# Rewriting the expert part of a two-block transformer kernel: a fixed order per pair of experts, a float32 gather from x, and eighteen weight places

## The chip, the cores and the metric

The kernel runs on one core of a Trainium2 chip, as one program. The metric is the device time of one execution in microseconds (us). Before the change three executions took 1468.20, 1471.01 and 1473.86 us; the median is 1471.01 us. The execution that the profiler recorded took 1472.58 us.

## What is computed

The input is 256 tokens of 1024 float32 features. Two layers of a first block (sparse attention, gated linear attention, spatial gating, and a feed-forward part) are followed by a second block: an attention layer and a mixture of 32 experts, of which each token uses two. The change concerns the mixture and the norm behind it.

```python
def hier_moe(h, w_group, b_group, w_router, b_router, w_e_gate, w_e_up, w_e_down):
    ...
    g_top = jnp.argmax(g_logits, axis=-1)                  # one of 4 groups
    ...
    e_w, e_idx = lax.top_k(jax.nn.softmax(e_logits, axis=-1), TOP_K)   # 2 of its 8 experts
    ...
    for e in range(N_EXPERTS):                             # 32
        a = jax.nn.silu(hf @ w_e_gate[e]) * (hf @ w_e_up[e])     # 1024 -> 512
        out = out + gates[:, e:e + 1].astype(hf.dtype) * (a @ w_e_down[e])   # 512 -> 1024
...
x = x + mixed @ w_out[l]
x = x + hier_moe(rmsnorm_2(x, g_ffn[l]), ...)
return rmsnorm_2(x, g_final)
```

The weights are float32. An expert has 6 MiB of them, the 32 experts together 201.3 MB.

## The kernel before

**Dense parts.** Everything ahead of the mixture multiplies by dense weights. SP's queue loads them into raw places of 8 KB per partition. ScalarE (ACT) casts each piece to a rounded high half `whi`, VectorE (DVE) subtracts to get the low half `wlo`, and TensorE (PE) makes three products of the halves with the halves of the activations (`h_hi`, `h_lo` and others). The tiles `x`, `h_hi`, `h_lo`, the raw places and the arena (one large tile that is cut into working tiles) stand in one pool, `con`; `whi` and `wlo` stand in the pool `split` behind it.

**The experts' weights.** The experts are taken in 16 pairs, q = 0 to 15. A pair has 12 units of 1 MiB: eight for the gate and up matrices (two experts, two matrices, two halves h of the 1024 rows) and four for the down matrices. `plan2` lists the units in the order in which SP loads them: the rows and the downs of a pair in turn, except that the rows of pair 15 stand ahead of the downs of pair 14. `Stream.pump` issues a load as soon as a place is free, and `Stream.free` gives a place back when PE has read it. Eight loads can be in flight, since an issue also waits for the load that is eight before it. The places are the 7 raw ones, 5 that `open_raw("right")` opens, 3 that `open_raw("left")` opens in the second half of `mix2` when `split` is closed, and `LENT` = 3 that `route` lends from the arena for one unit each: 18 units before any expert has run.

**The routing.** While `mix2` ends, `t_xg` makes transposed tokens for the router's logits, and rows of x times the gain (`xgr`) for the gather. `route` then picks each token's two experts by a chain of small VectorE operations. Between them `h_rows` scales `xgr` by the norm's factor and splits it into `h_hi` and `h_lo`, with GpSimd (POOL) and ACT.

**The experts' work.** Experts hold up to 32 tokens (`CAP`). For a batch of four pairs (8 experts) `t_batch` builds one-hot tables from the places, gathers the tokens by 32 products of `h_hi` and `h_lo` with them, builds gated one-hot tables by 24 small operations and transposes these for the way back (`gt`). A pair's gate and up products go into one psum bank of four 32-row strips, banks 4 and 5 in turn. `t_act` makes the activation and transposes it, `emit_down` does the down products into `Y`, and every second pair `emit_scatter` adds `Y` to the tokens in four psum banks. An `If` for experts with more than 32 tokens (`overflow`) stands in pair 15. `last_norm` ends the program.

**What sets the order.** The order is that of the instructions as they are recorded. `t_batch`, `t_act` and `t_most` are side tasks: at each `S.tick()` a planner (`Side`), with a clock of its own for each engine and the numbers of `LAST`, decides whether their next step is recorded; `S.until(...)` records the rest at the latest possible place. `emit_down(q - 1)` is recorded between the two halves of the rows of pair q.

All of these operations pass through one helper, so they carry the line number L257 in the profile; groups are told apart by their tiles.

## Time and profile before

| | |
|---|---|
| median of three executions | 1471.01 us (1468.20 to 1473.86) |
| the profiled execution | 1472.58 us |
| its span, first to last instruction | 1470.8 us |
| mean granted TensorE clock | 0.924 of full speed |
| busy: PE, DVE, ACT, POOL | 1294.8, 740.4, 558.8, 226.4 us |
| read from HBM | 358.1 MB, 244 GB/s over the span |
| the experts' weights | 201.3 MB, loaded from 932 to 1455 us |

The span falls into two parts. Up to about 975 us PE is busy nine tenths of the time or more and the DMA engines about half of it; from there on the DMA engines are busy nine tenths and PE about seven. The averages over the whole span hide this, so the stretches have to be read one at a time. [...]

### The profile page before, as it was taken

How to read it: one execution, taken by the hardware profiler on the slowest of the kernel's cores; microseconds unless marked ns; L12 is line 12 of the kernel's file. 1: busy time of each engine (PE TensorE's matmuls, PEld its weight loads, DVE VectorE, ACT ScalarE, POOL GpSimd, SP SyncE). 2: the span in 40 equal slices, each digit the busy share in tenths (PEclk: the TensorE clock that was granted, in tenths of full speed). 3: DMA queues.
4: the chain of work that ended last, by engine and by line, in shares of the span. 5: the costliest groups of instructions: out<-in, count | busy, mean ns of one | idle time of the engine just before them, and what ended most of it. 6: DMA issues, size and time to landing. Idle time of an engine off the chain costs nothing. (4 is left out here: it accounts for less than half of the span.)

```text
span 1470.8 us, 22896 instructions
## 1 busy us (share of the span) xinstructions
PE 1294.8 (88%) x8791; PEld 966.9 (66%) x8791; DVE 740.4 (50%) x1573; ACT 558.8 (38%) x1167; POOL 226.4 (15%) x348
## 2 busy tenths in 40 slices
PE   8989999999999999999999999978876857776576
PEld 8767999988777899988889999853323212311111
DVE  5587778756587677755766564663021200201001
ACT  5535655555526555555555455431000100100001
POOL 2154111101154111123332210120000000000000
PEclk9999999999999999999999999988987778787778
DMA  9551565556452566566435353697999899899995
GB/s 340 190 184 45 174 200 173 186 159 218 138 168 68 159 186 189 184 193 194 140 116 172 115 173 120 214 379 298 420 421 420 363 420 420 352 420 420 420 417 242
DMA packets 153558, 360.75 MB, mean 245 GB/s; under 512 B 8640, under 2 KB 98240, under 8 KB 128736
## 3 DMA queue, kind: packets, MB, share of 16 engines
q1 hardware_dynamic: 151328, 354.81, 66.1%
q0 software_dynamic: 1328, 3.63, 0.8%
q8 instruction: 71, 1.16, 0.3%
q10 hardware_dynamic: 784, 0.76, 0.2%
q14 instruction: 47, 0.39, 0.1%
HBM read 358.12 MB, written 1.05 MB: 244 GB/s over the span
## 5 line engine op out<-in xcount | busy, mean ns | idle before, releaser
L257 DVE TENSOR_TENSOR wlo<-raw,whi 128x512 fp32r<-128x512 f32 (+3 forms) x560 | 404.9, 730 | 255.4 <-ACT whi L257 243.2
L257 ACT CAST whi<-raw 128x512 fp32r<-128x512 f32 (+3 forms) x560 | 337.7, 606 | 341.6 <-PE psum L257 271.6
L257 PE MATMUL psum<-h_hi,whi 128*128 128x256 f32 x1040 | 296.0, 285 | 3.0 <-ACT whi L257 3.0
L257 PE MATMUL psum<-h_lo,whi 128*128 128x256 f32 x1040 | 290.6, 279 | 0.1
L257 PE MATMUL psum<-h_hi,wlo 128*128 128x256 f32 x1040 | 290.6, 279 | 0.2 <-DVE wlo L257 0.2
L257 PE MATMUL psum<-raw,arena 128*32 128x512 f32 x704 | 181.7, 696 | 58.9 <-DMA raw<-in_w_e_gate_dram 47.5
L257 DVE COPY arena<-psum 128x384 f32<-128x384 f32 (+4 forms) x68 | 38.1, 560 | 346.9 <-ACT arena L257 232.7
L257 PEld LDWEIGHTS psum<-h_hi,whi 128*128 128x128 f32 x1040 | 195.8, 188 | 10.1 <-issue 4.8
L257 PEld LDWEIGHTS psum<-h_lo,whi 128*128 128x128 f32 x1040 | 195.9, 188 | 0.9 <-issue 0.5
L257 PEld LDWEIGHTS psum<-h_hi,wlo 128*128 128x128 f32 x1040 | 195.8, 188 | 0.4 <-DVE wlo L257 0.4
L257 PE MATMUL psum<-raw_right,arena 128*32 128x512 f32 x496 | 143.8, 671 | 24.7 <-DMA raw_right<-in_w_e_gate_dram 17.1
L257 PE MATMUL psum<-whi,h_hi 128*128 128x256 f32 (+3 forms) x448 | 145.7, 325 | 1.4 <-ACT arena_o L257 1.1
L257 PE MATMUL psum<-whi,h_lo 128*128 128x256 f32 (+3 forms) x448 | 138.2, 308 | 0.0
L257 PE MATMUL psum<-wlo,h_hi 128*128 128x256 f32 (+3 forms) x448 | 138.1, 308 | 0.0
L257 PEld LDWEIGHTS psum<-raw,arena 128*32 128x32 f32 x704 | 38.8, 122 | 148.7 <-DMA raw<-in_w_e_gate_dram 62.5
L257 PE MATMUL psum<-raw_left,arena 128*32 128x512 f32 x312 | 110.3, 714 | 26.3 <-DMA raw_left<-in_w_e_gate_dram 20.4
L257 PE MATMUL psum<-arena 64*128 64x256 f32 (+10 forms) x668 | 115.4, 381 | 6.7 <-DVE arena L257 4.7
L257 ACT COPY arena<-psum 128x384 f32<-128x384 f32 (+3 forms) x61 | 32.0, 524 | 221.8 <-PE psum L257 212.4
L257 ACT ACTIVATE arena<-psum 128x256 f32<-128x256 f32 (+3 forms) x38 | 18.1, 476 | 240.7 <-PE psum L257 228.6
L257 POOL TENSOR_TENSOR arena<-arena 128x512 f32<-128x512 f32 (+2 forms) x46 | 49.2, 1079 | 295.6 <-DVE arena L257 286.6
L257 PEld LDWEIGHTS psum<-whi,h_hi 128*128 128x128 f32 x448 | 85.0, 190 | 11.0 <-issue 4.4
L257 PEld LDWEIGHTS psum<-arena 64*128 64x128 f32 (+4 forms) x668 | 63.0, 178 | 42.2 <-issue 22.1
(240 smaller groups left out, 1823.9 us busy)
## 6 DMA issues: line engine op xcount, KB each, us to landing
raw<-in_w_in_dram SPq DMA_DIRECT2D x60, 512.0 KB, 4.9
raw<-in_w_e_up_dram SPq DMA_DIRECT2D x30, 1024.0 KB, 19.8
raw<-in_w_e_down_dram SPq DMA_DIRECT2D x30, 1024.0 KB, 19.9
raw<-in_w_e_gate_dram SPq DMA_DIRECT2D x28, 1024.0 KB, 19.9
raw<-in_w_gate_dram SPq DMA_DIRECT2D x44, 512.0 KB, 4.0
raw<-in_w_up_dram SPq DMA_DIRECT2D x44, 512.0 KB, 5.0
raw_right<-in_w_e_down_dram SPq DMA_DIRECT2D x22, 1024.0 KB, 19.9
raw<-in_w_down_dram SPq DMA_DIRECT2D x20, 1024.0 KB, 5.1
```

The lines of the kernel that those rows point to most:

```text
L257: return f(*args, **kw)
```

## The change

The part from the router to the end is written anew.

- **Order.** The planner is no longer asked in the mixture. A pair is recorded as: rows of half 0, two side steps, rows of half 1, activation, two side steps, its transposes, one side step, its own down products, one side step. The side steps stand in a list: the one-hot tables, four gather steps, the norm factors, the gates (first batch only), two steps for the way back, and the scatters. The list of the next batch is added at the second pair of a batch (at the third pair in the first batch).
- **Gather.** It takes float32 `x` itself (two products of 256 columns per feature group, in float32, where there were four in rounded halves), the gain is applied as the result leaves psum, and the norm's factor of each gathered token is found by eight products with one column per batch and applied in the activation. `h_rows`, `xgr` and the loads of the gain for them are gone.
- **Way back.** The gated tables are made from the one-hot tables by 4 operations per half batch, instead of 24 per batch from the places.
- **Places.** `h_hi` and `h_lo` get a pool of their own, which is closed together with `split`, now at the start of `route`: 5 places instead of 3. The room of the router's tokens becomes another place for good, and `LENT` is 2: 18 places, and 20 units before any expert has run.
- **Warm products.** `route` records `WARM` = 5 float32 products of 512 columns of x whose result is not used, behind the router's logits.
- **Order of the loads.** Rows and downs alternate up to the end, and the last pair's downs are loaded as 8 units of 0.5 MiB (256 rows of 512 columns) so that the columns 0 to 511 come first.
- **End.** Down products, scatter and squares go by halves of the columns; the square's scale takes the place of a division; of the four last scalings ACT does one and DVE three. The final gain is loaded in pair 15, behind the `If`.
- **Addresses.** The arena loses 96 columns. `whi` and `wlo` start where they started (a tile `gap` of 56 columns sees to that); `h_hi` and `h_lo` start 109,512 bytes further on in each partition; x, the raw places and the arena move by 32 bytes modulo 64, or stay.

The core of the diff:

```diff
-LENT = 3
+WARM = 5
+LENT = 2
...
         for q in range(NQ):
             rows(q)
-            if q < NQ - 2:
-                down(q)
-        down(NQ - 2)
-        down(NQ - 1)
+            (down if q < NQ - 1 else last_down)(q)
...
         S.until(("xg", 0), ("xg", 1))
-        S.free = [7]
+
+        self.open_raw("left")
+        self.ar.drop(self.xg)
+        self.st.slots.append(self.room(2048))
         for _ in range(LENT):
-            self.st.lend(self.ar.now(2048), self.ar.drop)
+            self.st.lend(self.room(2048), self.ar.drop)
         self.st.pump()
+        for _ in range(WARM):
+            self.mm(self.ps(0), self.ident, self.x[:, 0, 0:512], True, True)
...
-        for tb in range(2):
-            self.h_rows(tb)
-        self.ar.drop(self.xgr, self.gffn)
...
+        def rows(k2):
+            xe = self.xe[b]
+            ps = self.ps(7 if b else k2).rearrange("p (k c) -> p k c", k=2)
             for i in range(2):
                 k = k2 * 2 + i
                 for tb in range(2):
-                    c0 = tb * D + (k // 4) * 512
-                    c = slice(c0 + k % 4, c0 + 512, 4)
-                    for h in (hi, lo):
-                        self.mm(ps[:, i * 256 : i * 256 + 256], h[:, c], d[:, tb, :], n == 0, n == 3)
+                    c0 = (k // 4) * 512
+                    self.mm(ps[:, i, :], self.x[:, tb, c0 + k % 4 : c0 + 512 : 4], d[:, tb, :], tb == 0, tb == 1)
+            gain = lambda k: self.gp[:, k // 4, k % 4 : k % 4 + 1]
+            k = k2 * 2
+            nc.scalar.activation(out=xe[:, k, :], in_=ps[:, 0, :], func=AF.Copy, scale=gain(k))
+            nc.vector.tensor_scalar(out=xe[:, k + 1, :], in0=ps[:, 1, :], scalar1=gain(k + 1), scalar2=None, op0=ALU.mult)
...
         for q in range(NQ):
...
+            self.emit_rows(q, 0)
+            if q == NQ - 1:
+                with self.tc.If(self.most > CAP):
+                    self.overflow()
...
+            side(2)
+            self.emit_rows(q, 1)
+            if q == 0:
+                side(1)
+            th = self.emit_act(q)
+            side(2)
             if q % 4 == 3:
+                side(99)
                 self.ar.drop(self.xe.pop(b))
+            at = self.emit_at(th)
+            side(1)
...
+            self.emit_down(q, at, None)
+            self.ar.drop(at)
+            if q % 2:
+                todo[:0] = [lambda quad=q // 2, c=c: self.emit_scatter(quad, c) for c in range(2)]
+            side(1)
+        self.last_norm(at)
...
+    def last_norm(self, at):
         for c in range(2):
+            self.emit_down(NQ - 1, at, c)
+            self.emit_scatter(NQ // 2 - 1, c)
             for tb in range(2):
                 ps = self.ps(c * 2 + tb)
-                nc.scalar.activation(out=self.ps(7), in_=ps, func=AF.Square, accum_out=self.ssq[:, tb, c : c + 1])
+                nc.scalar.activation(
+                    out=self.ps(7), in_=ps, func=AF.Square, scale=D ** -0.5, accum_out=self.ssq[:, tb, c : c + 1]
+                )
...
-                if c == 0:
+                if c + tb == 0:
                     nc.scalar.activation(out=o, in_=o, func=AF.Copy, scale=r)
...
-            n = 3
+            self.close("h")
+            n = 5
...
-        N_RAW, N_SPLIT, ARENA = 7, 6, 12032
+        N_RAW, N_SPLIT, ARENA = 7, 6, 11936
```

The order on PE, at the start of the experts, before. `wr` is the router's matrix, `s_9417` the choice of experts, `raw_83` and the like are places with weights; of each run of like rows the first stand here.

```order
L257 MATMUL psum<-wr,arena 128x36 x8
L257 MATMUL psum<-s_9417,tab_67 128x64
L257 MATMUL psum<-s_9417,ones 128x32
L257 MATMUL psum<-onehot,h_hi 128x256
L257 MATMUL psum<-onehot,h_lo 128x256
...
L257 MATMUL psum<-raw_83,arena 32x512
L257 MATMUL psum<-raw_87,arena 32x512
...
L257 MATMUL psum<-onehot,h_hi 128x256
```

And after:

```order
L258 MATMUL psum<-wr,arena 128x36 x8
L258 MATMUL psum<-x,tab_67 128x512 x5
L258 MATMUL psum<-s_9425,tab_67 128x64
L258 MATMUL psum<-s_9425,ones 128x32
L258 MATMUL psum<-onehot,x 128x256 x8
L258 MATMUL psum<-raw_81,arena 32x512
...
L258 MATMUL psum<-onehot,x 128x256 x8
L258 MATMUL psum<-raw_right_9167,arena 32x512
...
L258 MATMUL psum<-rstd,onehot 64x1 x8
L258 MATMUL psum<-tab_67,arena 128x128 x4
```

Before, 16 gather products stand ahead of the first 8 expert products, 8 more gathers and 8 more expert products follow, and then 8 gathers. After, the five warm products stand between the router and the choice; 8 gathers are followed by all 16 expert products of half 0, and 8 more by those of half 1.

The order on PE at the gather of a later batch, before (`tab_67` is the identity of the transposes, `arena 128x512` the scatter):

```order
L257 MATMUL psum<-arena 128x512 x4
L257 MATMUL psum<-raw_left_9340,arena 32x512
...
L257 MATMUL psum<-onehot,h_hi 128x256
...
L257 MATMUL psum<-raw_left_9340,arena 32x512
...
L257 MATMUL psum<-onehot,h_lo 128x256
L257 MATMUL psum<-tab_67,arena 128x128 x8
L257 MATMUL psum<-tab_67,arena 128x64 x4
L257 MATMUL psum<-raw_right_9163,arena 32x512
```

And the gather of a later batch after:

```order
L258 MATMUL psum<-onehot,x 128x256 x8
L258 MATMUL psum<-tab_67,arena 128x64 x4
L258 MATMUL psum<-onehot,x 128x256 x4
L258 MATMUL psum<-raw_left_9371,arena 32x512
...
L258 MATMUL psum<-arena 128x512 x2
L258 MATMUL psum<-raw_left_9375,arena 32x512
...
L258 MATMUL psum<-arena 128x512 x2
L258 MATMUL psum<-rstd,onehot 64x1 x8
L258 MATMUL psum<-raw_85,arena 32x512
...
L258 MATMUL psum<-tab_67,arena 128x128 x8
```

Before, 24 of the batch's 32 gather products stand in one row behind the rows of a pair, directly followed by all transposes of the way back; after, the gathers stand in lots of 4 and 8 between the expert products, and the transposes come a pair later, with expert products between.

The order on PE at the end of the program, before and after:

```order
L257 MATMUL psum<-tab_67,arena 128x64 x4
L257 MATMUL psum<-raw_left_9340,arena 32x512
L257 MATMUL psum<-raw_left_9341,arena 32x512
...
L257 MATMUL psum<-raw_right_9167,arena 32x512
L257 MATMUL psum<-raw_left_9339,arena 32x512
...
L257 MATMUL psum<-arena 128x512 x4
```

```order
L258 MATMUL psum<-tab_67,arena 128x64 x4
L258 MATMUL psum<-raw_right_9169,arena 32x512
L258 MATMUL psum<-raw_right_9170,arena 32x512
...
L258 MATMUL psum<-arena 128x512 x2
L258 MATMUL psum<-raw_83,arena 32x512
L258 MATMUL psum<-raw_84,arena 32x512
...
L258 MATMUL psum<-arena 128x512 x2
```

Before, the scatter's four products follow all down products of the last pair; after, two of them stand between the down products of the two column halves and two behind them.

## Rows read from the trace of the kernel before

**Rows 1.** The page: DMA share (tenths) and GB/s in 40 slices of the span.

```profile
DMA  9551565556452566566435353697999899899995
GB/s 340 190 184 45 174 200 173 186 159 218 138 168 68 159 186 189 184 193 194 140 116 172 115 173 120 214 379 298 420 421 420 363 420 420 352 420 420 420 417 242
```

**Rows 2.** Stretches: us, busy PE PEld DVE ACT POOL, PEclk, DMA share, GB/s.

```profile
975.00:980.00 5.00, 4.20 (x21) 2.89 (x20) 2.25 (x4) 1.45 (x4) 0.39 (x3) 1.00 0.48 141
980.00:990.00 10.00, 2.35 (x16) 2.21 (x16) 8.51 (x21) 3.14 (x3) 6.47 (x4) 0.56 1.01 427
990.00:1005.00 15.00, 13.26 (x67) 9.37 (x68) 2.55 (x10) 1.47 (x4) 0.00 (x0) 0.73 0.34 127
1005.00:1145.00 140.00, 103.59 (x571) 39.92 (x571) 31.77 (x107) 10.90 (x20) 0.00 (x0) 0.84 1.01 419
1145.00:1155.00 10.00, 8.54 (x56) 2.58 (x60) 1.60 (x3) 0.96 (x2) 0.00 (x0) 0.66 0.57 209
1270.00:1280.00 10.00, 7.56 (x48) 2.28 (x52) 1.91 (x4) 1.18 (x3) 0.00 (x0) 0.59 0.47 167
```

**Rows 3.** SP's queue in order of time: start, us, operation (an issue).

```profile
980.34 0.42 SPq L257 DMA_DIRECT2D arena<-in_w_e_up_dram  x1
1003.38 0.33 SPq L257 DMA_DIRECT2D raw<-in_w_e_gate_dram  x1
1130.35 0.38 SPq L257 DMA_DIRECT2D raw_right<-in_w_e_gate_dram  x1
1150.89 0.33 SPq L257 DMA_DIRECT2D raw_right<-in_w_e_up_dram  x1
```

**Rows 4.** PE in order of time, from the router to the first freed place.

```profile
979.87 2.48 PE L257 MATMUL psum<-wr,arena 128*128 128x36 f32 x16 [0.35 <-DVE arena L257]
...
990.88 0.69 PE L257 MATMUL psum<-s,tab 128*128 128x64 f32 x2 [8.53 <-DVE s L257]
...
992.80 0.57 PE L257 MATMUL psum<-onehot,h_hi 128*128 128x256 f32 x1 [0.87 <-DVE onehot L257]
...
996.85 2.58 PE L257 MATMUL psum<-raw,arena 128*32 128x512 f32 x16
...
1001.45 1.92 PE L257 MATMUL psum<-raw,arena 128*32 128x512 f32 x16
```

**Rows 5.** DVE in order of time, in the routing chain.

```profile
984.66 1.74 DVE L257 TENSOR_TENSOR tt<-el,top8a 128x16 f32<-128x16 f32 x1
986.43 2.26 DVE L257 TENSOR_TENSOR tt<-tt,tab 128x16 f32<-128x16 f32 x1
...
989.55 0.17 DVE L257 TENSOR_TENSOR tt<-e,top8b 128x16 f32<-128x16 f32 x1
```

**Rows 6.** POOL in order of time, in the same stretch.

```profile
984.02 4.65 POOL L257 TENSOR_TENSOR h_lo<-arena,h_hi 128x1024 fp32r<-128x1024 f32 x2 [1.16 <-ACT h_hi L257]
```

**Rows 7.** Weight loads by form, 990 to 1130 us: count, busy us, mean ns.

```profile
L257 PEld LDWEIGHTS psum<-onehot,h_hi 128*128 128x128 f32 x39 | 12.7, 326 | 8.4 <-issue 8.4
...
L257 PEld LDWEIGHTS psum<-arena 128*128 128x128 f32 x16 | 2.9, 191 | 3.7 <-issue 3.7
```

**Rows 8.** DVE in order of time, the gated tables of a later batch.

```profile
1137.69 5.04 DVE L257 TENSOR_SCALAR arena<-tab,place,g 128x32 f32<-128x32 f32 x24
```

**Rows 9.** PE in order of time, behind those tables.

```profile
1145.99 0.74 PE L257 MATMUL psum<-tab,arena 64*128 64x64 f32 x4 [2.16 <-DVE arena L257]
1147.20 3.64 PE L257 MATMUL psum<-raw_right,arena 128*32 128x512 f32 x16 [0.47 <-ACT arena L257]
```

**Rows 10.** A stretch at the program's start, columns as above.

```profile
4.00:44.00 40.00, 36.63 (x231) 32.95 (x231) 23.71 (x46) 24.36 (x51) 6.89 (x13) 0.96 1.06 363
```

**Rows 11.** The chain that ended last, its last steps: start, us, step.

```profile
1455.12 3.22 PE psum L257 x14
...
1458.99 3.72 PE psum L257 x8
...
1466.04 0.72 ACT arena L257
```

More of the change, by code (lines that the diff above doesn't have):

```diff
@@ new lines, in side_batch, with most_steps, first, second @@
+        steps = [places] + [lambda k2=k2: rows(k2) for k2 in range(4)] + [scales]
+        if b == 0:
+            steps.append(lambda: self.gates())
+        return steps + [lambda pr=pr: back(pr) for pr in range(2)]
+    def most_steps(self):
+        nc = self.nc
+        V = nc.vector
+        pm, m1 = self.small([P, 1], "pm", bufs=1), self.small([1, 1], "m1", bufs=1)
+        mi = self.sm.tile([1, 1], mybir.dt.int32, tag="mi", name="mi", bufs=1)
+        def first():
+            V.tensor_reduce(out=pm, in_=self.place.rearrange("p t e -> p (t e)"), axis=AX.X, op=ALU.max)
+        def second():
+            ps = self.ps(7)[0:1, 0:P]
+            self.tr(ps, pm)
+            V.tensor_reduce(out=m1, in_=ps, axis=AX.X, op=ALU.max)
+            V.tensor_copy(out=mi, in_=m1)
+        def third():
+            self.most = nc.values_load(mi[0:1, 0:1], min_val=0, max_val=T)
+        return [first, second, third]
@@ L2206, in t_act, with emit_act @@
+    def emit_act(self, q):
+        nc = self.nc
+        gu = self.ps(4)
+        rh, r2 = (t[:, q % 4 : q % 4 + 1] for t in self.re[q // 4])
+        th = self.room(512)
+        nc.scalar.activation(out=th[0:64], in_=gu[0:64], func=AF.Tanh, scale=rh)
         nc.vector.scalar_tensor_tensor(
```

337 lines of the change are left out of this document (145 added, 192 removed).

## The prediction

> **What bounds the kernel now.** I read the page's 40 slices first, to split the span: up to slice 26 the DMA engines are half idle, and from slice 28 on they run at 420 GB/s with few dips [rows 1]. The dense parts, up to about 975 us, are bound by PE; the change leaves their instructions nearly alone. Then I cut the experts' part into stretches with their DMA share [rows 2]: between the dips the share is 1.01 at 419 GB/s while PE is busy for 103.6 of 140 us. So the weights' stream bounds this part, and a unit of 1.05 MB takes 2.50 us at 420 GB/s. What a change of order can win there is the idle time of the DMA engines, the missing share times the length [rows 2]: 5 x 0.52 = 2.6 us at 975, 15 x 0.66 = 9.9 us at 990, 10 x 0.43 = 4.3 us at 1145, 10 x 0.53 = 5.3 us at 1270. Together 22.1 us. Third, SP's queue says why: no load is issued between 980.3 and 1003.4 us, until PE has freed the first four places [rows 3], and again none between 1130.4 and 1150.9. Fourth, the chain of waits tells the end: from the last down products at 1455.1 to the last scaling at 1466.0 us, then the store, to 1470.8 [rows 11].
>
> **The start of the experts.** Before, the first place is freed behind the second lot of expert products, near 1003.4 us. Three things move this.
>
> First, the routing chain. Two of its VectorE steps took 1.74 and 2.26 us where their like takes 0.17 [rows 5]; they lie beside POOL's 4.65 us of `h_lo` [rows 6], which goes. 1.74 + 2.26 - 0.34 = 3.7 us less, so the choice on PE that began at 990.88 [rows 4] could begin at 987.2. In its way stand the five warm products, which PE takes from 982.4 us (979.87 + 2.48 [rows 4]). A float32 product of 512 columns is two instructions; 8 such instructions took 3.72 us in the scatter [rows 11], 0.46 each, so ten take 4.6 us at the full clock, to 987.0, and up to twice that, 991.7, at half of it. PE comes from the dense products at clock 1.00 and the next stretch has 0.56 with an idle PE [rows 2], so I take a time between, 988.5.
>
> Second, the gather. Before, 16 instructions from 992.80 to 996.85 [rows 4], 0.25 us each, then products, 8 more gathers, products; after, the first half needs 8 float32 products, also 16 instructions, then 32 instructions of expert products in a row, (2.58 + 1.92) together [rows 4]. The 8 gathers between (about 2.0 us) move behind the first freed places. From the choice to the first free place: 1.9 (992.80 - 990.88) + 4.0 + 0.7 for the eviction + 4.5 = 11.1 us, and 988.5 + 11.1 = 999.6. Bounds: 998.3 with no cost of the warm products, 1002.8 with the worst.
>
> Third, the cover. 20 units instead of 18 are issued before any place is needed, 2 x 2.5 = 5.0 us more of streaming. The stream ran dry about 9.9 us before 1003.4, near 993.7; now near 998.7, if the new places are open as early. Three of the 18 came from `mix2`'s end, five plus the router's room come at the start of `route` now: these wait for the same last dense product and for the router's at 982.4, and eight units of work are in flight by then, so no time is lost. The hole is 999.6 - 998.7 = 0.9 us plus a fresh start of the stream of 1 us or so: I take 1.7 us of 9.9, a gain of 8.2. Bounds: 9.9 (no hole) and 5.0 (1002.8 + 1 - 998.7 = 5.1 us of hole left, so 4.8; the cover alone).
>
> Of the 2.6 us at 975, nothing is won: the places still wait for `mix2`.
>
> Weight columns are read from x with a step of 4 elements, as from `h_hi` before. There the weight load took 326 ns against 191 ns without a step [rows 7], yet 16 gathers went by in 0.25 us each [rows 4], so the load lay beside the neighbouring product. I count nothing; if it came to the front, (0.33 - 0.25) x 32 = 2.6 us per batch, 1.3 us before the first free place. [...]
>
> **The two later dips.** The one at 1145 follows from the lump: a batch's gathers without expert products between, then PE waiting for the 24 small operations of 5.04 us [rows 8] and for the activation behind them (2.16 us at one wait, and the transposes end only at 1147.2 [rows 9]). From 1130.4 us on no load is issued for 20.5 us [rows 3]; the eight in flight cover 8 x 2.5 = 20 us less what had run by then. After, no row of side steps stands longer than 8 gathers and 4 transposes, and three more places cover 7.5 us more. Both dips, 4.3 + 5.3 = 9.6 us, go; bounds 9.6 and 0 (the order on PE could make an equal lump where a batch's last steps are forced behind the fourth pair). I take 9.2.
>
> What must hold for this: PE's work per pair below the 12 x 2.5 = 30.0 us of its weights. Expert products are 6 lots of 16 instructions; a lot takes 1.92 us at the full clock [rows 4] and 3.64 at the lower one [rows 9], so 11.5 or 21.8 us. The gather adds 32 x 0.25 / 4 = 2.0, the scatter 3.72 / 2 = 1.9, transposes and the activation's waits some 3.5. Full clock: 18.9 us; half of it: 21.8 + 4.0 + 3.7 + 4 = 33.5. The clock of 0.84 from 1005 to 1145 [rows 2] lies between and gives about 24. It holds, with the lower clock as the point where it would not.
>
> **The last pair.** 8 units of 0.5 MB have rows of 2 KB. At the program's start loads with such rows ran at a share of 1.06 and 363 GB/s [rows 10], against 419. For 4.2 MB that is 11.6 against 10.0 us: a cost of 1.6; from 0 to 2, I take 1.4. [...]
>
> **The end.** The products behind the last load stay four steps of two strips. The scatter there halves, 3.72 to 1.86 [rows 11], its other half lies beside the last loads; the halves' squares lie with it. Of the scalings, ACT's second, 0.72 us at 1466.04, goes to DVE beside ACT's first: 0.4 us, about half of it, since DVE then has three. Gain 2.2 us, bounds 1 and 3.5.
>
> **The dense parts.** The order on PE is the same but for two places at the end of the mixers of the first block's layers, where the smaller arena moves some temporaries; nothing says which is better: 0, from -4 to +4. `h_hi` and `h_lo` lie elsewhere, which no row prices; if products ran 0.7% quicker or slower, 975 us would give 7 either way.
>
> **The sum**, against the profiled execution (1472.6, of which the span is 1470.8): 1472.6 - 8.2 - 9.2 + 1.4 - 2.2 + 0 = 1454.4. The median is 1.6 below that execution, so 1452.8; I say 1453.
>
> **The rivals.**
> - *The start keeps most of its hole*: the warm products run at the lower clock and the new places open late. Gain there 4.8 or less, the rest as above: about 1457 to 1462. For it: clock 0.56 at 980 to 990; against: PE's 1.00 just before.
> - *PE becomes the bound.* Float32 products at the lower clock need 33.5 us per pair; if the steadier, thinner work left the clock at 0.50 throughout, 16 x 3.5 = 56 us come on top of the gains: about 1508, slower. It decides where a pair passes 30.0 us. For it: stretches at 0.59 and 0.66 [rows 2]; against: these are the ones where PE waited.
> - *The dips move instead of going*: with the fixed order PE waits in each pair for the activation ahead of its own downs, and places come in bursts. If every batch keeps a hole of 4 to 5 us, 16 to 20 us are back: 1465 to 1472, no change. Against: 18 places are 1.5 pairs.
> - *The addresses do more than they should*, that is, the dense operands' places are not the same in what matters: 2% of 975 us is 19.5, slower than or equal to before, 1465 to 1480; the good side of it gives 1435 to 1445.
>
> **How the numbers follow.** Forecast 0.62 (own range 1446 to 1459), kept hole 0.13, dense part quicker 0.07, dips that move 0.07, dense part slower 0.07, PE the bound 0.04. A measurement here tells about 0.5%, 7.4 us, from no change. Faster, below 1463.6: 0.62 + 0.13 + 0.07 and a part of the two middle ones, 0.86. Same 0.07, slower 0.07. Range 1443 to 1466: it leaves out the two tails.
>
> **What would show it.** In the stretch 990 to 1005 a DMA share of 0.85 or more, and 1.0 all the way to the end; the choice on PE near 988; no issue of SP waiting more than 4 us for a place; the last landing near 1439 and 13 to 14 us of the span behind it. Wrong if PE's waits for weights vanish in the experts' part (PE the bound), if the stretch up to 975 us differs by over 4 us, or if idle DMA time over 5 us stands in any stretch of a pair.

## The result, and the profile after

The changed kernel takes 1456.26 us (median of four, 1453.80 to 1457.22) against 1471.47 us before on the same chip: a ratio of 0.9896, with a 95% interval of 0.9873 to 0.9919. Forecast were 1453 and a range of 1443 to 1466. The profiled execution took 1456.56 us with a span of 1454.8 us, 16.0 us less than before. So the change is worth about 1%, clear of the noise. Timed again beside later experiments, the same kernel gave 0.9926 (0.9900 to 0.9953), so differences of 3 us between kernels of different sets of runs prove nothing; below, verdicts rest on the traces.

The two rows of the page that answer to [rows 1]:

```profile
DMA  9651556555534456557434454479999999999995
GB/s 341 193 173 49 157 185 192 176 187 175 177 109 139 140 180 192 171 189 229 146 114 149 127 164 145 157 308 414 418 420 421 420 421 421 420 421 421 421 419 205
```

From slice 27 on (the first slice is number 0) there is no dip until the last, in which the loads have ended. The stretches say the same; here are those of [rows 2] with one ahead and two behind them (columns as there; PEclk is the clock that TensorE was granted, as a share of the full one, so that "the lower clock" is 0.50, and DMA share is the mean busy share of the 16 DMA engines):

```profile
950.00:975.00 25.00, 24.75 (x121) 20.02 (x120) 16.39 (x29) 11.68 (x24) 4.01 (x4) 1.00 0.87 346
975.00:980.00 5.00, 5.00 (x27) 4.20 (x27) 0.00 (x0) 0.00 (x0) 0.00 (x0) 1.00 0.59 246
980.00:990.00 10.00, 8.70 (x40) 5.00 (x38) 6.80 (x28) 1.45 (x4) 1.09 (x3) 1.00 0.83 324
990.00:1005.00 15.00, 14.22 (x75) 10.06 (x79) 2.48 (x7) 2.09 (x6) 0.00 (x0) 0.89 1.01 413
1145.00:1155.00 10.00, 8.56 (x60) 2.87 (x54) 0.15 (x1) 0.17 (x1) 0.00 (x0) 1.00 1.01 419
1270.00:1280.00 10.00, 6.83 (x49) 2.19 (x48) 1.11 (x3) 0.85 (x2) 0.00 (x0) 1.00 1.01 421
1430.00:1432.00 2.00, 0.66 (x4) 0.55 (x4) 0.83 (x2) 0.23 (x1) 0.00 (x0) 1.00 1.05 384
1434.00:1436.00 2.00, 2.00 (x6) 0.37 (x4) 0.00 (x0) 0.00 (x0) 0.00 (x0) 0.50 0.52 197
```

Counted as missing GB/s against 420, the holes at 990, 1145 and 1270 were 10.5, 5.0 and 6.0 us before and are 0.3, 0 and 0 now (by the DMA share, which the prediction used, they were 9.9, 4.3 and 5.3). The pause at `mix2`'s end, 3.3 us before (141 GB/s for 5 us), is now spread over 975 to 990 and is 4.4 us.

The last weights land at about 1435.4 us, where before it was about 1453.2. Here and below, this is the time at which the DMA engines fall under half busy; the last packets come some 1.3 us later in both:

```profile
1452.00:1454.00 2.00, 1.12 (x5) 0.14 (x2) 0.00 (x0) 0.00 (x0) 0.00 (x0) 1.00 0.42 172
```

(this line is of the kernel before). So the weights are in 17.8 us earlier, but the span ends only 16.0 us earlier: the end behind the last landing grew from 17.6 to 19.4 us. The chain of waits of the kernel after shows it (start, us, step), to be read against [rows 11]:

```profile
1425.03 3.63 PE psum L258 x26
1430.12 0.76 DVE arena L258
1432.21 5.35 PE psum L258 x16
1438.21 5.57 PE psum L258 x20
1444.54 2.00 PE psum L258 x4
```

Before, the chain's last long wait was for a landing at 1455.1, and what followed was one unit's products. Now no step behind 1425.03 waits for a load: the last rows of pair 15 are multiplied, activated, and then the two column halves follow one another on PE, the second of them long after its weights are there.

How the two later dips went can be read from PE. Before, from the last products of one pair's rows to the next product on weights, which frees places again [rows 9], it did this:

```profile
1128.90 0.51 PE L257 MATMUL psum<-onehot,h_hi 128*128 128x256 f32 x1
...
1138.66 0.47 PE L257 MATMUL psum<-tab,arena 128*128 128x128 f32 x1 [1.68 <-DVE arena L257]
1141.13 0.90 PE L257 MATMUL psum<-tab,arena 128*128 128x128 f32 x3 [2.00 <-DVE arena L257]
```

and after, in the same place:

```profile
1128.08 2.24 PE L258 MATMUL psum<-onehot,x 128*128 128x256 f32 x8
...
1136.89 3.64 PE L258 MATMUL psum<-raw_left,arena 128*32 128x512 f32 x32
```

Before, PE had no product on weights for 18.3 us (1128.90 to 1147.20): 8 us for 24 gather instructions, the rest for VectorE's tables of the way back, their transposes, and the activation behind them. After, it is 8.8 us (1128.08 to 1136.89), with as many gather instructions and the pair's own transposes in it. So the gathers stand as thick as before; what left the row is the way back, which comes a pair later and takes VectorE 8 operations (1.5 us) instead of 24 (5.04 us).

The routing, on PE and on VectorE (answers to [rows 4] and [rows 5]):

```profile
983.10 1.98 PE L258 MATMUL psum<-wr,arena 128*128 128x36 f32 x16 [0.34 <-DVE arena L258]
984.91 4.54 PE L258 MATMUL psum<-x,tab 128*128 128x512 f32 x10
989.95 0.43 PE L258 MATMUL psum<-s,tab 128*128 128x64 f32 x2 [0.51 <-DVE s L258]
...
991.36 5.64 PE L258 MATMUL psum<-onehot,x 128*128 128x256 f32 x16 [0.78 <-DVE onehot L258]
996.92 3.64 PE L258 MATMUL psum<-raw,arena 128*32 128x512 f32 x32
1000.49 4.11 PE L258 MATMUL psum<-onehot,x 128*128 128x256 f32 x16
```

```profile
987.39 0.17 DVE L258 TENSOR_TENSOR tt<-el,top8a 128x16 f32<-128x16 f32 x1
987.60 0.17 DVE L258 TENSOR_TENSOR tt<-tt,tab 128x16 f32<-128x16 f32 x1
```

The two steps of 1.74 and 2.26 us take 0.17 each. From the router's first product to the choice it is 6.85 us (11.01 before), to the first free place 17.5 us (1000.57 against 983.10; 23.5 before). The router itself comes 3.2 us later than before (983.10 against 979.87): the dense parts became slower.

### The profile page after: what moved, and what is told of

It is laid out like the page before. It is cut to its first block, busy times and chain, and to the rows that moved or that the text cites. A ratio compares the mean times of both kernels' runs of the same rounds, so it can differ in the third digit from the quotient of the medians.

```text
span 1454.8 us, 23003 instructions
## 1 busy us (share of the span) xinstructions
PE 1312.3 (90%) x8865; PEld 977.7 (67%) x8865; DVE 724.5 (50%) x1521; ACT 559.5 (38%) x1175; POOL 215.8 (15%) x345
## 4 chain that ended last, share of the span: by engine, by line
PE 36%; DMA 27%; DVE 3%; ACT 2%; POOL 1%; issue 1%; SPq 0%; POOLq 0%; DVEq 0%; ACTq 0%
PE psum L258 36%; DMA raw_right<-in_w_e_up_dram 7%; DMA raw<-in_w_e_up_dram 5%; DMA raw<-in_w_e_down_dram 5%; DMA raw_left<-in_w_e_down_dram 4%; DMA raw_left<-in_w_e_up_dram 3%; DMA arena<-in_w_e_up_dram 3%; ACT whi L258 1%; DVE wlo L258 1%; DVE arena L258 1%; POOL arena L258 1%; ACT arena L258 1%; DVE arena_o L258 0%; ACT psum L258 0%; ACT arena_o L258 0%
## 5 line engine op out<-in xcount | busy, mean ns | idle before, releaser
L258 PE MATMUL psum<-arena 64*128 64x128 f32 (+10 forms) x740 | 153.8, 412 | 19.7 <-DVE arena L258 8.2
L258 PE MATMUL psum<-raw,arena 128*32 128x512 f32 x604 | 143.4, 705 | 23.0 <-DMA raw<-in_w_e_gate_dram 12.9
L258 PE MATMUL psum<-raw_right,arena 128*32 128x512 f32 x428 | 105.8, 702 | 20.7 <-DMA raw_right<-in_w_e_up_dram 10.7
L258 PEld LDWEIGHTS psum<-arena 64*128 64x128 f32 (+4 forms) x740 | 71.5, 176 | 69.1 <-issue 25.1
L258 DVE SCALAR_TENSOR_TENSOR arena<-arena,psum 128x256 f32<-128x256 f32 (+2 forms) x36 | 17.8, 517 | 201.0 <-ACT arena L258 198.1
L258 PE MATMUL psum<-raw_left,arena 128*32 128x512 f32 x408 | 95.6, 693 | 13.6 <-DMA raw_left<-in_w_e_gate_dram 8.9
L258 PEld LDWEIGHTS psum<-wlo,h_hi 128*128 128x128 f32 x448 | 85.4, 191 | 4.6 <-issue 1.4
L258 PEld LDWEIGHTS psum<-raw,arena 128*32 128x32 f32 x604 | 31.2, 125 | 85.3 <-issue 48.4
L258 PEld LDWEIGHTS psum<-whi,h_lo 128*128 128x128 f32 x448 | 85.3, 190 | 4.5 <-DVE h_lo L258 0.2
```

Source lines behind the costliest of these rows:

```text
L258: return f(*args, **kw)
```

## The experiments

Since that dense part wanders by some us from profile to profile for reasons of its own (below), I compare "router to end": from the first of the router's last 16 products to the end of the span. It is 490.9 us before, and 471.7 and 472.0 in two profiles of the changed kernel. That these two agree is partly chance: the last four row products of pair 15 begin 441.9 and 444.0 us behind the router, and from there to the end it is 29.8 us with TensorE partly at the lower clock (0.50 from 1434 to 1436) and 28.0 us at the full one (1.00 from 1426 to 1448). So a difference of less than 2 us is not taken as shown below, and a larger one only with the lines that account for it.

### The old order of the last two pairs

```diff
         for q in range(NQ):
             rows(q)
-            (down if q < NQ - 1 else last_down)(q)
+            if q < NQ - 2:
+                down(q)
+        down(NQ - 2)
+        last_down(NQ - 1)
...
+            if q == NQ - 2:
+                at14 = at
+                continue
             if q == NQ - 1:
+                self.emit_down(q - 1, at14, None)
+                self.ar.drop(at14)
                 break
```

> The changed kernel with the order of the last two pairs put back as it was: loads rows 14, rows 15, downs 14, downs 15 (still in eight half units by columns), and on PE rows 15 ahead of downs 14. Theory 'chain from the last rows': in the changed kernel the last weights land near 1435 us but PE is then still busy with what began when the rows of pair 15 landed at 1425.0 (rest of the rows, activation to 1432.2, down products of column half 0, scatter, half 1, scatter), so the end is 19.5 us behind the last landing. With the rows 10 us earlier the last landing bounds again: 5 to 7 us faster than the changed kernel, about 1450. Rival 'landing': the end follows the last landing by a fixed tail and 2 KB rows cost what they cost: no change, within 1.5 us.

Measured: 1454.33 us, ratio 0.9897 (0.9877 to 0.9917); router to end 470.0 us, 1.7 less than the changed kernel, which is within the scatter. Not the 5 to 7 us of my theory; the rival's "no change" stands, though not for its reason. PE in order of time shows three things in the way:

```profile
1414.05 1.89 PE L258 MATMUL psum<-raw_left,arena 128*32 128x512 f32 x2 [4.55 <-PEq L2333]
1419.37 1.01 PE L258 MATMUL psum<-raw,arena 128*32 128x512 f32 x1 [3.44 <-issue]
...
1432.70 2.33 PE L258 MATMUL psum<-raw_right,arena 128*32 128x512 f32 x9 [1.43 <-DVE arena L258]
```

The first products behind the `If` (line 2333 of this kernel, 1414.05) waited 4.6 us for it, the next start another 3.4 us later at 1419.37, with no wait that the profile shows; and at 1432.70 the last pair's downs wait 1.4 us until the psum bank of the pair before is copied. The order alone doesn't shorten the chain.

### The last downs whole

```diff
-            (down if q < NQ - 1 else last_down)(q)
+            down(q)
...
+        self.emit_down(NQ - 1, at, None)
         for c in range(2):
-            self.emit_down(NQ - 1, at, c)
             self.emit_scatter(NQ // 2 - 1, c)
```

> The changed kernel with the last pair's downs loaded as four units of 1 MB and multiplied in four strips at once, then the scatter of both halves, as before the change; the order of the loads stays rows 15, downs 15. Theory 'chain from the last rows': two strips at a time make the 32 down instructions take 16 steps, four strips 8; the scatter could start near 1437.5 with both halves and end near 1441.5 where the changed kernel ends its second at 1446.5: 4 to 6 us faster than the changed kernel, about 1451. Rival (as the prediction had it): going by halves saves 2.2 us at the end and costs 0.7 to 1.4 us in the loads, so taking it back costs 1 to 1.5 us: about 1457.5.

Measured: 1454.01 us, ratio 0.9900 (0.9880 to 0.9919), span 1451.8; router to end 468.5 us, 3.2 less than the changed kernel. Its end on PE:

```profile
1431.92 5.33 PE L258 MATMUL psum<-raw_right,arena 128*32 128x512 f32 x18 [0.53 <-ACT arena L258]
...
1439.61 3.70 PE L258 MATMUL psum<-arena 128*128 128x512 f32 x8 [0.70 <-ACT arena L258]
```

All down products and the whole scatter are over at 1443.3, where the changed kernel's second scatter ends at 1446.5, though the eight steps ran partly at the lower clock (0.50 from 1431 to 1437), as the changed kernel's did (0.50 from 1434 to 1436). Of the 3.2 us about 1 is in the loads, which run at 410 to 418 GB/s from 1428 to 1431 as whole units and at 381 to 387 as half units. Going by halves costs 3 us here, where the prediction had it save 2.2 less 1.4 for the loads. The rival (slower by 1 to 1.5) falls. The 2 us in the medians are inside the scatter between sets of runs.

### Fifteen places

```diff
-LENT = 2
+LENT = 3
...
-        self.st.slots.append(self.room(2048))
...
-            self.close("h")
-            n = 5
+            n = 3
```

and `h_hi`, `h_lo` back in the pool `con`, a `gap` of 96 columns behind the arena.

> The changed kernel with 15 places and 3 lent ones, as before the change (left pool of 3, no place in the router's room), and with h_hi and h_lo back at their old address. Theory 'order': the later dips went because the side steps are spread; with 18 units the stream runs dry near 998 and PE frees the first places near 1000.5, so a hole of 3 to 5 us comes back at the start and under 1 us at 1145 and 1270: 2 to 4 us more in the experts' part. Rival 'places': the dips at 1145 and 1270 come back as they were, 4 to 5 us each: 10 us or more. The dense parts: the changed kernel's loads fall behind by 0.7 us and 0.95 us during the gate and up products of the two layers, and by 0.4 us during each of the down products; theory 'address' expects these 2.5 us gone, rival 'smaller arena' expects them unchanged. The steps of +3 and -2 us at the ends of the mixers are from the smaller arena's order by both and stay. In sum 1454 to 1458 by 'order', 1462 or more by 'places'.

Measured: 1461.06 us, ratio 0.9945 (0.9928 to 0.9961). The stretches:

```profile
986.00:1005.00 19.00, 17.71 (x91) 11.77 (x94) 6.62 (x30) 1.74 (x6) 0.00 (x0) 1.00 0.88 354
1145.00:1155.00 10.00, 8.65 (x44) 2.62 (x44) 0.68 (x1) 0.58 (x1) 0.00 (x0) 1.00 1.01 420
1270.00:1280.00 10.00, 8.55 (x56) 2.86 (x52) 0.15 (x1) 0.17 (x1) 0.00 (x0) 1.00 1.01 417
```

The later dips do not return: the new order and its lighter side steps remove them with the old number of places. No run separates these two. At the start a hole of 3.0 us is back (19 x 66 / 420), and router to end is 3.6 us longer. "Order" holds for the dips, "places" for the rest of the start. The time lies above the range of "order" because the first expert load came 5.0 us later than before, where the changed kernel's came 3.5 later; the dense parts are told below.

### Without the warm products

```diff
-WARM = 5
+WARM = 0
```

> The changed kernel without the five warm products. Theory: the choice of experts waits for VectorE, not for these products (PE waited 0.5 us behind them), so it starts when it did; gathers and first expert products run at a clock nearer to 0.5 and free the first places 2 to 4 us later, near 1003 to 1004, when the stream of 20 units runs dry near 1003: a hole of 0 to 3 us, 0 to 2 us slower than the changed kernel. Rival: they are in the way, and without them it is 1 us faster.

Measured: 1455.73 us, ratio 0.9907 (0.9889 to 0.9925); router to end 471.2 us, no difference. From the router (983.98) to the choice it is 6.85 us again, and the first gathers take 5.58 us:

```profile
990.83 0.69 PE L258 MATMUL psum<-s,tab 128*128 128x64 f32 x2 [4.87 <-DVE s L258]
...
992.67 5.58 PE L258 MATMUL psum<-onehot,x 128*128 128x256 f32 x16 [0.78 <-DVE onehot L258]
```

With the warm products the same gathers took 5.6 us in about half of the profiles of kernels that have them (5.62 to 5.64 in six), 4.11 in five, and 6.55 in the one with POOL's work, so PE kept the clock in some profiles and not in others (granted 0.60 and 0.55 from 992 to 996 us in the changed kernel, 1.00 from 990 to 1000 in the run with whole downs and early places), and here the stream hides either. Theory and rival both expected a little; neither is shown.

### The arena at its old size

```diff
-        N_RAW, N_SPLIT, ARENA = 7, 6, 11936
+        N_RAW, N_SPLIT, ARENA = 7, 6, 12032
```

(and a `gap` of 24 columns for 56).

> The changed kernel with the arena at its old size (12032 columns), which gives PE the old order everywhere ahead of the experts; h_hi and h_lo stay at their new address. In the changed kernel the loads fall 3.0 us behind at the end of the first layer's mixers and gain 0.6 to 2 us at the second's, and fall behind by 0.74 us in each layer's gate and up products and 0.41 us in each layer's down products. Theory: the two steps at the mixers come from the order and go (within 0.5 us of before each); the 0.74 us come from the address and stay. Rival: all of it comes from the addresses and stays. In time: 1 to 2 us faster than the changed kernel, 1453 to 1455, by the theory; no change by the rival.

Measured: 1457.58 us, ratio 0.9917 (0.9891 to 0.9943); router to end 470.7 us. My theory falls for the first layer: with the old order on PE the loads are again 3.7 us late behind its mixers. For the second layer's mixers it holds in this one profile: the step there is +0.1, and -0.8 to -3.3 us in the other twelve. The 0.74 us of the gate and up products became 0.52 and 0.47. The rival does not hold as it was put either; what the stretches show stands at the end of this section.

### The early places

```diff
             if c == 1:
                 self.ar.drop(mx)
+                for _ in range(2):
+                    self.st.lend(self.room(2048), self.ar.drop)
+                self.st.pump()
...
-LENT = 2
+LENT = 0
```

> The changed kernel with its two lent places opened in mix2, where the mixed activations are dropped, instead of in the routing: two units can be loaded while mix2 still runs. Theory: the changed kernel's stream stands still from 977.8 to 982.6 us, since all new places wait for mix2's last product; with two more the stream runs on there, but the 20 units are then loaded by 998 and the first place comes free at 1000.6, so 3 us are given back: 1 to 2.5 us faster than the changed kernel. Rival: the rooms come free only with mix2's end and nothing changes.

Measured: 1452.98 us (1449.73 to 1459.98), ratio 0.9889 (0.9862 to 0.9915), where the changed kernel on the same chip had 0.9926 (0.9900 to 0.9953); the intervals overlap.

```profile
990.00:1000.00 10.00, 8.72 (x45) 5.94 (x48) 2.54 (x10) 1.25 (x4) 0.00 (x0) 0.83 0.87 361
1000.00:1005.00 5.00, 5.00 (x28) 3.94 (x20) 0.48 (x1) 0.47 (x1) 0.00 (x0) 1.00 0.58 195
```

The pause at 976 to 982 is gone (418 and 414 GB/s there) and a hole of 1.4 + 2.7 us stands at 998 instead, as expected: nearly all of what the early places win is given back, because the number of units ahead of the first free place is the same. The profile, which is of the slowest of the six executions, shows no gain: the last four row products of pair 15 begin 441.5 us behind the router, as in the changed kernel, and router to end is 474.5 us, 2.8 more, with TensorE at a granted clock of 0.66 from 1420 to 1440 where the changed kernel had 0.91. So the better median is not accounted for by this trace.

### Three edits at the end, with the If and without it

The old order as above, and:

```diff
-        y = self.ps(6)
+        y = self.ps(6 if c is None else 4)
...
             self.emit_rows(q, 0)
-            if q == NQ - 1:
-                with self.tc.If(self.most > CAP):
-                    self.overflow()
...
             if q == NQ - 1:
+                with self.tc.If(self.most > CAP):
+                    self.overflow()
                 self.emit_down(q - 1, at14, None)
```

> As the run with the old order of the last two pairs, and in addition the If stands behind the last pair's transposes instead of between its rows (where PE stood for 3.4 us), and the last pair's down products get a psum bank of their own, so that they don't wait 1.4 us for the copy of the pair before. Theory 'PE's chain at the end': the changed kernel ends 19.5 us behind its last landing because PE's chain from the last rows is longer than the loads behind them; with these three edits the products of the second column half end near 1438, 2 to 3 us behind the last landing at 1435, and the end follows 11 us later: about 1449, 4 to 6 us faster than the changed kernel. Rival: the half-wise products and scatters keep the chain as long as it was, 1 us as in the run with the old order alone.

Measured: 1457.25 us, ratio 0.9921 (0.9895 to 0.9946); the end is 20.1 us behind the last landing, router to end 472.6 us. Nothing won; the rival's number, but not its reason:

```profile
1420.85 0.66 PE L258 MATMUL psum<-tab,arena 64*128 64x64 f32 x4 [2.36 <-DVE arena L258]
1427.48 3.38 PE L258 MATMUL psum<-raw,arena 128*32 128x512 f32 x16 [5.97 <-PEq L2352]
```

PE stands 6.0 us, and what releases it is its own sequencer at the line of the `If`. The next run takes the `If` out (its two lines, nothing else).

> As the run with three edits at the end (old order of the last two pairs, own psum bank), without the If and its branch for experts with more than 32 tokens, which these inputs don't take: that part of the computation is left out. Theory 'If': in that run PE stood for 6.0 us at the If, behind the last transposes, from 1421.5 to 1427.5, while the downs of pair 14 were there; this wait ate what the new order won. Without it the products of the last column half end 4 to 5 us earlier, 2 to 3 us behind the last landing: 4 to 5 us less behind the last landing than the changed kernel (which ends 19.5 us behind it), 1449 to 1452. Rival: the down products of two pairs in a row are the chain, and the end stays 19 to 20 us behind the last landing.

Measured: 1454.05 us, ratio 0.9877 (0.9853 to 0.9901). The end is 15.1 us behind the last landing (1437.5 to 1452.6), router to end 467.0 us, 5.6 less than with the `If` and 4.7 less than the changed kernel. PE there:

```profile
1425.49 0.66 PE L258 MATMUL psum<-tab,arena 64*128 64x64 f32 x4 [2.36 <-DVE arena L258]
1426.09 1.92 PE L258 MATMUL psum<-raw,arena 128*32 128x512 f32 x16
```

No wait of note between the transposes and the downs. The 4.4 us less behind the last landing are what the theory asked for; its 1449 to 1452 us were missed, since the first expert load came 5.7 us later than before. That the `If` is what stood in the way at this place is shown (6.0 us with it, no wait of note without); what PE's sequencer does at it in that time is not. In the changed kernel the `If` costs nothing: PE stands 0.4 us at it and then waits for weights twice (0.9 us at 1422.50, 1.5 at 1425.03).

```profile
1420.62 1.02 PE L258 MATMUL psum<-raw,arena 128*32 128x512 f32 x2 [0.39 <-PEq L2330]
```

### Whole downs and early places together

> The changed kernel with the two edits that gave something apart: the last pair's downs whole (four strips at once), and the two lent places opened in mix2. Theory: the whole downs took 3 us off the end in the profile, the early places 1 to 2 us: 1450 to 1453, 0.985 to 0.989 of the time before. Rival: nothing beyond the changed kernel, 0.990 to 0.993.

(Edits: those of "the last downs whole" and "the early places".) Measured: 1451.84 us (1450.30 to 1453.20), ratio 0.9867 (0.9844 to 0.9890), span 1449.0; router to end 465.6 us, 6.1 less than the changed kernel. It beats the kernel before clearly, and the changed kernel by 6 us in the trace and by some 0.3 to 0.6% in the ratios, whose intervals overlap. Against "the last downs whole" alone (468.5) it is 2.9 us less, and the trace says why the early places give more here than by themselves: the first gathers ran at the full clock (4.11 us, 5.63 there), the first place came 15.9 us behind the router instead of 17.5, and the hole behind the router is 2.3 us instead of 4.1. That the clock decides this is read from two profiles, one of each.

### POOL's work back beside the routing

```diff
+        junk = self.room(1024)
+        for _ in range(2):
+            nc.gpsimd.tensor_tensor(out=junk, in0=self.x[:, 0], in1=self.x[:, 1], op=ALU.subtract)
+        self.ar.drop(junk)
         for _ in range(WARM):
```

> The changed kernel with POOL's two subtractions of 128x1024 put back beside the routing chain (on x, with a result that is not used). Theory: in the kernel before, two steps of VectorE's chain took 1.74 and 2.26 us instead of 0.17 because POOL's 4.65 us lay beside them; so some steps take that long again and the choice on PE starts 10 to 10.6 us behind the router's products instead of 6.85. The stream of 20 units runs dry then for 1 to 3 us: 1 to 3 us slower than the changed kernel. Rival: the two slow steps came from something else (ACT's casts, the order of the chain), the steps stay at 0.17 and nothing changes.

Measured: 1455.96 us, ratio 0.9897 (0.9873 to 0.9921); router to end 472.1 us. POOL and VectorE:

```profile
981.34 4.78 POOL L258 TENSOR_TENSOR arena<-x 128x1024 f32<-128x1024 f32 x2
```

```profile
983.23 0.47 DVE L258 TENSOR_TENSOR tt<-lg,top4a 128x8 f32<-128x8 f32 x1
983.74 0.17 DVE L258 TENSOR_TENSOR tt<-tt,tab 128x8 f32<-128x8 f32 x1
...
984.13 2.01 DVE L258 TENSOR_TENSOR oh4a<-tt,tf 128x8 f32<-128x8 f32 x1
```

Two steps are slow again, though not the same two as before: one ends at 983.70, the other at 986.14, which is, to 0.03 us, when POOL's first and second subtraction end (981.34 to 986.12, 2.39 each). The choice comes 9.0 us behind the router, 2.15 later, where I had expected 10 to 10.6. The cause of the slow steps is shown. In the time nothing can be told: the first place comes later (20.7 us behind the router), the stream has a hole of 2.7 us (192 GB/s from 1000 to 1005), and the last four row products of pair 15 begin 444.1 us behind the router, 2.1 later than in the changed kernel's first profile and as in its second; the end ran at the full clock (1.00 from 1426 to 1444) and gave that back.

### More work for PE

```diff
             self.ar.drop(at)
+            for _ in range(4):
+                self.mm(self.ps(5), self.ident, self.x[:, 0, 0:512], True, True)
```

> The changed kernel with four more float32 products of 512 columns on PE in each pair but the last (results not used), 3.4 us of PE per pair at the full clock and up to 6.8 at the lower one, 51 to 100 us in all. Theory 'stream': the weights' loads bound the pairs, PE is busy for 337 of 443 us there, so nothing changes, within 2 us. Rival 'PE': PE's chain per pair is near its 30 us, and the time grows by 1 us or more per pair, 15 us or more.

Measured: 1458.23 us, ratio 0.9912 (0.9890 to 0.9934); router to end 472.1 us. From 1010 to 1420 PE is busy 339.1 us (309.9 in the changed kernel) and the stream is as full:

```profile
1010.00:1420.00 410.00, 339.09 (x1833) 122.48 (x1834) 47.12 (x100) 32.50 (x63) 0.61 (x1) 0.91 1.01 420
```

60 more products cost nothing that can be seen. The pairs are bound by the stream, and PE has room for at least these four products in each.

### The dense parts, over all runs

The loads' issue times, compared with the kernel before, give the dense parts' delay stage by stage. In two profiles of the changed kernel and eleven of its variants it is between -0.4 and +6.3 us at the first expert load (3.5 and 2.6 in the changed kernel). The largest step that all have is the end of the first layer's mixers, +1.7 to +4.0 us. Stretches there, before, then after, then with the old arena (columns as above):

```profile
110.00:115.00 5.00, 4.67 (x30) 3.87 (x30) 3.71 (x24) 4.00 (x19) 2.98 (x8) 0.66 0.43 132
120.00:125.00 5.00, 3.46 (x28) 2.79 (x28) 4.29 (x17) 1.96 (x8) 5.00 (x12) 1.00 0.00 0
125.00:130.00 5.00, 5.00 (x47) 4.09 (x47) 4.90 (x19) 3.89 (x13) 4.10 (x11) 1.00 0.01 3
```

```profile
115.00:120.00 5.00, 2.30 (x19) 1.41 (x17) 4.92 (x30) 4.76 (x21) 1.94 (x1) 0.86 0.00 0
120.00:125.00 5.00, 5.00 (x24) 5.00 (x25) 4.71 (x17) 0.60 (x2) 5.00 (x11) 0.50 0.00 0
```

```profile
120.00:125.00 5.00, 3.35 (x25) 2.79 (x26) 3.80 (x14) 2.33 (x9) 5.00 (x8) 0.94 0.00 0
125.00:130.00 5.00, 5.00 (x26) 4.23 (x26) 3.85 (x14) 0.96 (x3) 4.43 (x11) 0.50 0.00 0
```

The granted clock falls to 0.50 here in every profile, in that of before too (from 110 to 115), but for different lengths. Between 95 and 141 us the lower clock takes 1.7 us of full-clock time in the profile of before (5 x 0.34, first line above). In the others the step goes with what it takes: +1.7 us where that is 3.4 and 3.9 us, +2.9 to +3.2 where it is 5.1 or 5.2 (+3.7 with the old arena), +4.0 where it is 8.5. Ten of these thirteen profiles are of the same instructions at the same addresses up to here, so the length changes from one execution to the next. That the size of the step is the clock's is shown; whether other executions of the kernel before fall as long can't be told from its one profile. With the old order PE is busy 3.35 of 5 us where it was 3.46 before, and the clock fell behind it all the same.

The smaller steps are steady, and the clock was 1.00 throughout there: 0.74 us in each layer's gate and up products in every kernel with the changed layout, 0.1 with `h_hi` and `h_lo` back in front, 0.5 with the old arena, 0.83 in the kernel without the `If`, whose tiles all lie 96 bytes lower. So they go with addresses, up to 0.9% of these 93 us; which property of an address decides stays open. (In the changed kernel `h_hi` starts 109,568 bytes further on than before, at 141,632 against 32,064, not 109,512; with fifteen places it starts 160 bytes behind its old address, not at it; with the old arena it starts 384 bytes and `whi` 256 bytes behind the changed kernel's.)

## Why the prediction was right, and where it was not

Term by term, in us:

| step | predicted | measured |
|---|---|---|
| start of the experts | -8.2 | -10.2 at 990 to 1005, +1.1 at 975 to 990 |
| later dips | -9.2 | -11.0 |
| half units of the last pair | +1.4 | +0.9 (385 against 420 GB/s for 4.2 MB) |
| the end | -2.2 | +1.8 |
| dense parts | 0 | +3.2 at the router, of which +2.1 in the stream at 975 (346 against 381 GB/s for 25 us) |
| sum | -18.2 | -15.3 by these, with 2.1 for the dense parts; the span fell by 16.0 |

The first two rows are measured in missing GB/s, the forecasts in DMA share; by the share the holes that went were 9.9 and 9.6 us, so there the forecasts were closer than the table makes them. That the time came within 4 us of the forecast is partly luck: the start, the dips and the half units came out 3.2 us better, the end and the dense parts 6.1 us worse. Two sums of the prediction are a little off, and neither moves the forecast: 1003.4 - 9.9 is 993.5, not 993.7, and the dips that move, 16 to 20 us on top of 1453, would give 1469 to 1473, not 1465 to 1472.

*The start* was right in mechanism. The choice came 6.85 us behind the router, by VectorE's chain and not, as I had it, by the warm products (8.6). The slow steps were POOL's, as said, and the run with POOL's work shows it. The hole went altogether, since the first place came 17.5 us behind the router instead of the 19.7 forecast. What was missed is the pause at `mix2`'s end, which I took as unchanged; it grew by 1.1 us, and not because `mix2` ended later: measured from the router it is 3.3 us before and 4.3 after. With the two lent places opened in `mix2` it is gone.

*The dips* went since the lump was broken up, as said, but not quite as said. The prediction had "no row of side steps stands longer than 8 gathers and 4 transposes"; in truth 12 gathers (24 instructions) and 4 transposes stand in a row, 8.8 us, and what made the difference is that the way back left the row and got lighter. The three more places were not needed for the dips, only for the start. *PE as the bound* is ruled out by 60 added products that cost nothing. *The kept hole* and *the dips that move* did not come. *The dense part slower* came to a part: 3.2 us, not the 20 us of that rival, and mostly by the clock.

*The strided gather*: after, 16 gather instructions took 4.11 us at the full clock, 0.25 each, and half of the scatter's 0.46 for twice the columns is 0.23, so little is lost and nothing had to be counted. But the reading behind it was wrong. The 0.25 us of before were read in a stretch at the lower clock (0.50 from 992 to 997), and at the full clock (1.00 from 999.7 to 1001.2) the gathers of before were no quicker:

```profile
999.71 0.40 PE L257 MATMUL psum<-onehot,h_lo 128*128 128x256 f32 x1
...
1001.12 0.40 PE L257 MATMUL psum<-onehot,h_lo 128*128 128x256 f32 x1
```

These two are six starts apart, 0.235 us each, as at 993 to 996 us, while rounded products of 280 columns with weights in a row started every 0.13 us at the full clock (94.81 to 95.33). So the step of 4 did slow the gathers before; float32 products, which take longer (0.25), hide it. The weight loads point the same way: before, those of the gathers, with the step, took 326 and 331 ns on average (`h_hi`, `h_lo`), those of the dense products of halves, also 128x128 and with weights in a row, 188 to 190; after, the gathers' loads from x took 327.

*The end* is the step that failed. "The products behind the last load stay four steps of two strips. The scatter there halves ... its other half lies beside the last loads" took for granted that the last landing still bounds the end; the sign named for it, 13 to 14 us of the span behind the last landing, failed with 19.4. Before, the rows of the last pair were loaded ahead of the downs of pair 14, so that everything but one unit's products was done when the last weights landed. With rows and downs in turn, the rows of pair 15 land 10 us before the end of the stream, and behind them PE has the activation (3.5 us), two column halves that use two strips of four and so take twice the steps (16 products from 1440.13 to 1443.76, 3.63 us, where 32 in four strips take 3.64 at 1136.89), two copies and two scatters in a row: 21.5 us from 1425.03 to 1446.5. The runs put some 3 us on the halves, about 1 of it in the loads. The old order with its own psum bank gives 4.7 us with the `If` out of its way, though the changed kernel's first profile had part of its end at the lower clock (its first column half took 5.35 us there and 3.65 in the second profile); with the `If`, nothing. The `If` alone, taken out of the changed kernel, was not run, but there PE waits for weights behind it.

## What to carry to other kernels

A stage that is bound by a stream of weights is judged by the missing bandwidth of each stretch, and here order and places did different work: taking the longest row of side steps apart, and making it lighter, removed the dips (11.0 us), with 15 places too; the number of units before the first freed place set the hole at the start (0.3 us with 20 units, 3.0 us with 18). Where a stream ends, ask again what bounds: work out the chain from each of the last loads, not from the last one alone, with the strips that each product uses. And a control-flow block whose body is skipped had a price here, 0.4 to 6.0 us of an idle PE by its place: put it where its engine waits anyway.

## What the runs showed of the hardware

- The `If`, whose long body is skipped, kept PE idle for 6.0 us in one place and 4.6 in another, and for 0.4 us where the changed kernel has it; taking it out of the first gave 5.6 us from the router to the end.
- Beside two GpSimd subtractions of 128x1024, two steps of VectorE's routing chain took 0.47 and 2.01 us (1.74 and 2.26 us in the kernel before), where their like took 0.17, and ended with them to 0.03 us (to 0.06 us in the kernel before); others of the chain ran between at 0.17 us.
- Loads of half a megabyte with rows of 2 KB ran at 381 to 387 GB/s from 1428 to 1431 us in the changed kernel while the stream was full, whole units at 410 to 418 in the same stretch of another run. The 363 of the program's start were measured over other loads too.
- Rounded products of 256 columns with weights read at a step of 4 elements started every 0.235 us at either clock (1.00 and 0.50), where weights in a row allowed 0.13 us for 280 columns at the full clock; float32 products of 256 columns with the step started every 0.25.
- The same gate and up products at the same granted clock (1.00) took 0.1 to 0.83 us longer of 93, up to 0.9%, when their operands lay elsewhere.
